# A hybrid decoder layer on one core: tile addresses, one wide value split, memory taken from two ends, and blocks staged through DRAM

## The chip, the core and the metric

The kernel runs on one core of one Trainium2 chip. The metric is the device time of one execution in microseconds (us). Three runs of the kernel before took 2890.93, 2891.61 and 2895.39 us; their median is 2891.61 us. The engines are PE (TensorE, with its weight loads shown as PEld), DVE (VectorE), ACT (ScalarE), POOL (GpSimd) and SP, which here only issues DMAs.

## The reference

One decoder layer on x of 2048 tokens by 1024, in float32:

```
u  = x * (1 + s1) + sh1                     # modulation vectors from c
qa, ka, va, qb, kb, vb, ga, gb = split(u @ w_in)
ya = banded attention, 8 heads, window 128, with sinks
yb = three dilated groups of 4 heads (dilation 1, 4, 16), mixed by their denominators
m  = (sigmoid(ga) * (ya @ w_a) + sigmoid(gb) * (yb @ w_b)) @ w_o
x1 = layer_norm(2**0.25 * x + g1 * m)
u2 = x1 * (1 + s2) + sh2
out = layer_norm(2**0.25 * x1 + g2 * ((silu(u2 @ w_gate) * (u2 @ w_up)) @ w_down))
```

w_gate and w_up are 1024 x 2816, w_down is 2816 x 1024.

## The kernel before, in words

Each float32 operand of a product is split into a high and a low part (`split`, L114: a copy on ScalarE, L115, then a subtraction on VectorE, L116), and each product is three matmuls (`PASS`, L141). PE works through five stages in one stream.

1. **The dilated groups** (L622 to L679). Four residue classes r, for each first the group of dilation 4 (g = 2), then that of 16. For g = 2 `project_v` (L553) makes the values of both groups at once, 4 PSUM banks of 512 columns (8 heads). `split_v` (L569) splits the first four heads of all four banks into three bfloat16 parts (`v_split`, L361: a ScalarE copy L364, then on VectorE L365, L366, L367); after that `send_v` (L578) splits the other four heads and stores them to DRAM, from where `fetch_v` loads them for the other group. The banks carry the name mm, of which there are four, and the next projection needs one.
2. **The near group and branch A** (L681 to L751), four chunks of 512 tokens.
3. **Merge, output projection, first layer norm** (L772 to L919), chunks in the order 3, 0, 1, 2. mT (pool mtp, L777) is the stationary operand of the output projection (L903). The rows x1 go to DRAM (x1_s).
4. **The first two products of the FFN** (L940 to L1130), in a Strassen form with seven products for each 2 x 2 block. Two passes p of 1024 tokens, in each eleven groups g of 256 columns, for each group one set of products with w_gate and one with w_up: 44 sets of 84 matmuls (L1014). `left(p, k)` (L956), for k = 0 to 3, loads four 512 x 128 blocks of x1, transposes them on PE (L967), modulates them on ScalarE (L968), forms four sums (`left_sums`, L928) and splits the seven blocks into comb tiles. `Right` (L976) loads 1 MB of weights (raw), forms four sums (`right_sums`, L934) and splits them into four units a to d, which replace the units of the set before as its products end. At the end of an up set `left_sums` runs on GpSimd over the four blocks of the gated result, and the seven blocks are stored to h_s (L1129, L1130). raw, sums, gated results and left blocks share one pool, g4, of six 1 MB tiles. The first and the last set of a pass (`set_by_block`, L1079) go block by block k, so that they can run while `left` makes the blocks.
5. **The product with w_down** (L1132 to L1268): seven products m in the order 1, 2, 6, 5, 3, 7, 4, eleven steps each; a step loads and splits one pair of factors (`factors`, L1147) and issues 24 matmuls (L1171) into eight banks. In the steps of m = 1 `right_of` (L1160) makes the sums of w_down and stores them to t_s. After m = 3 `first_half`, after m = 7 `second_half` (L1223, L1232) run one token block per step: the gate g2 on GpSimd (L1190), the residual (L1191), statistics and layer norm on VectorE. The last six factor pairs of m = 4 are held, and each block t is finished and stored on its own (L1265).

All DMAs are issued by SP, in order. The tile framework places each tile in its pool, the pools of a stage one after another from the low end of memory, makes an instruction that takes over a tile wait for the last user of the memory, and orders the work of each engine by its own estimate of when it is ready.

Of the kernel before, what the change touches and what calls it, by code (L numbers as in the profile page):

```python
# [23 lines left out]
KT = D // 128  # L24
# [28 lines left out]
def tile_pool(tc, name, bufs, stack):  # L53
    return stack.enter_context(tc.tile_pool(name=name, bufs=bufs, reuse_waits="tile"))
# [3 lines left out]
def trunk(ctx, tc, x, c, w_ada, b_ada, w_in, sinks, w_a, w_b, w_o, ln1_g, ln1_b,  # L58
# [17 lines left out]
    t_s = dram.tile([FT // 2, 4, 128, 512], F32, name="t_s")  # L76
# [15 lines left out]

    early = ctx.enter_context(ExitStack())
# [3 lines left out]
    ubp = early.enter_context(tc.tile_pool(name="ubp", bufs=UB))  # L97
    utp = early.enter_context(tc.tile_pool(name="utp", bufs=20))
    qp = early.enter_context(tc.tile_pool(name="qp", bufs=12))
# [261 lines left out]
    def v_split(pool, v, ps, nh, h0=0):  # L361
        pv = ps[:, h0 * 64:(h0 + nh) * 64].rearrange("p (h d) -> p h d", h=nh)
        r = pool.tile([128, 6, 64], F32, name="vr")[:, :nh]
# [37 lines left out]
    with ExitStack() as ph:  # L401
# [90 lines left out]
        vrp = pool("vrp", 1)  # L492
        att = pool("att", 3)
        at = Attention()
# [74 lines left out]
        def split_v(ps, nh):  # L569
            res = []  # L570
            for t in range(4):
                v = ring(vp, 8, [128, 6, 3, 64], BF16, "v")
# [5 lines left out]
        def send_v(ps, r):  # L578

            for t in range(4):  # L580
# [3 lines left out]
                nc.sync.dma_start(v_s[r, t * 128:(t + 1) * 128], v[:, :4].rearrange("p h a d -> p (h a d)"))  # L584

        def fetch_v(r):
            res = []
            for a in range(4):
                v = ring(vp, 8, [128, 6, 3, 64], BF16, "v")
# [32 lines left out]
        with ExitStack() as ph1:  # L622
            tab, osp, ada = pool("tab1", 1, ph1), pool("osp", 4, ph1), pool("ada", 1, ph1)
            vtp = pool("vtp", 2, ph1)
# [56 lines left out]
        with ExitStack() as ph2:  # L681
            tab, ogp, ytp = pool("tab2", 1, ph2), pool("ogp", 2, ph2), pool("ytp", 2, ph2)
            ptp = pool("pt2", PTB, ph2)
            at.phase = 1
            tA = bias_tables(tab, ubp, "tab", 127, [(h, 1) for h in range(8)])
# [85 lines left out]

    with ExitStack() as ph:  # L772
        ada = pool("ada3", 1, ph)
        tmp = pool("tmp3", 2, ph)
        ylp = pool("ylp", 4, ph)
        xrp = pool("xrp", 4, ph)
        mtp = pool("mtp", 16, ph)  # L777
        sgp = pool("sgp", 3, ph)
        later = ada_steps(ada, (S2, SH2, G2))
# [61 lines left out]

        yls, yT = [], []
        for _ in chain(y_rows(3, yls), y_T(yls, yT)):
            pass
        for ch, after in ((3, 0), (0, 1), (1, 2), (2, None)):
            mT, yls = [], []
            rows = y_rows(after, yls) if after is not None else iter(())
            for m in range(KT):
# [21 lines left out]
                if m >= 4:  # L870
# [10 lines left out]
            turn = [0, False]  # L881

            def bank():

                turn[0] += 1
                if turn[1]:
                    return psum.tile([128, 512], F32, name="mm")
                return psum.tile([128, 512], F32, name="so"[turn[0] % 2], bufs=2)

# [26 lines left out]
            for b in range(4):  # L916
                layer_norm(tmp, xr[b], sts[b], l1g, l1b)
                T = ch * 4 + b
                nc.sync.dma_start(x1_s[T * 128:(T + 1) * 128, :], xr[b])  # L919

    early.close()
    pool = partial(tile_pool, tc)
    A11, A12, A22, A_1, A_2, A_3, A_4 = range(7)
    G = FT // 2

    def left_sums(s, a11, a12, a21, a22, eng):  # L928
        eng.tensor_tensor(s[:, 0], a21, a22, op=OP.add)  # L929
        eng.tensor_tensor(s[:, 1], s[:, 0], a11, op=OP.subtract)  # L930
        eng.tensor_tensor(s[:, 2], a11, a21, op=OP.subtract)
# [362 lines left out]
```

## Time and profile before

| | |
|---|---|
| median of 3 runs | 2891.61 us |
| the profiled execution, time | 2895.43 us |
| its span, first to last instruction | 2893.4 us |
| granted TensorE clock, mean | 0.97 |
| PE busy | 2723.8 us |
| DVE busy | 1957.7 us |
| ACT busy | 1157.5 us |
| POOL busy | 254.9 us |
| HBM read, written | 325.94 MB, 94.97 MB |

The profile counts an engine as busy from the start of an instruction to its end; "idle before" is the engine's idle time just before an instruction and what released it. A granted clock of 1.00 is the full 2.4 GHz, one of 0.50 is 1.2 GHz; a stretch's number is its mean.

### The profile page before, as it was taken

The numbers are of one execution on the slowest core, as the hardware profiler recorded it, in microseconds if no ns is written. First come the engines' busy times: TensorE is split into PE (matmuls) and PEld (weight loads), VectorE is DVE, ScalarE is ACT, GpSimd is POOL, SyncE is SP. The second block draws the span as 40 slices with busy tenths as digits, with TensorE's granted clock in tenths as the row PEclk, the third lists the DMA queues.
The fourth block names the chain that finished last, engine by engine and source line by source line (L and its number), as shares of the span: only waits on it lengthen the run. The fifth ranks groups of instructions, "written<-read, shape, count | busy, mean of one in ns | idle before, by whom it ended". The sixth has DMA issues, their size and how long they took to land. (4 is left out here: it accounts for less than half of the span.)

```text
span 2893.4 us, 36361 instructions
## 1 busy us (share of the span) xinstructions
PE 2723.8 (94%) x13331; PEld 2232.6 (77%) x13331; DVE 1957.7 (68%) x3459; ACT 1157.5 (40%) x1918; POOL 254.9 (9%) x163
## 2 busy tenths in 40 slices
PE   7899999999999999999978999996999997999986
PEld 5677778888887888888856888885888886888875
DVE  7756677787769867655467666666666674543499
ACT  3544655666685343342224222233322222333220
POOL 0000000000000000000000111101111110000233
PEclk9999999999999999999989999997999998999998
DMA  9855857776788664734423233232332325974463
GB/s 282 227 154 143 212 143 165 153 171 146 167 223 269 212 182 129 229 120 153 126 80 97 97 109 104 93 117 86 109 107 97 110 95 218 325 266 150 136 221 125
DMA packets 570306, 459.23 MB, mean 159 GB/s; under 512 B 206152, under 2 KB 482704, under 8 KB 570128
## 3 DMA queue, kind: packets, MB, share of 16 engines
q1 hardware_dynamic: 570128, 456.92, 54.1%
q8 instruction: 104, 1.70, 0.2%
q14 instruction: 74, 0.61, 0.1%
HBM read 325.94 MB, written 94.97 MB: 145 GB/s over the span
## 5 line engine op out<-in xcount | busy, mean ns | idle before, releaser
L1014 PE MATMUL mm<-cb,w 128*128 128x512 f32 x3696 | 861.8, 395 | 31.4 <-ACT w L115 12.3
L1014 PEld LDWEIGHTS mm<-cb,w 128*128 128x128 f32 x3696 | 700.1, 190 | 184.5 <-ACT w L115 13.4
L148 PE MATMUL mm<-ut,whl 128*128 128x512 f32 x3072 | 736.2, 396 | 24.0 <-DVE vr L365 16.8
L148 PEld LDWEIGHTS mm<-ut,whl 128*128 128x128 f32 x3072 | 576.5, 190 | 156.0 <-issue 18.4
L1171 PE MATMUL acc<-hw 128*128 128x512 f32 x1848 | 427.2, 394 | 37.6 <-ACT hw L115 18.7
L1171 PEld LDWEIGHTS acc<-hw 128*128 128x128 f32 x1848 | 351.4, 191 | 113.4 <-ACT hw L115 29.5
L116 DVE TENSOR_TENSOR whl<-raw,whl 128x1024 fp32r<-128x1024 f32 (+1 forms) x228 | 265.5, 1165 | 164.6 <-ACT whl L115 162.9
L115 ACT ACTIVATE whl<-raw 128x1024 fp32r<-128x1024 f32 (+1 forms) x228 | 230.3, 1010 | 330.8 <-PE mm L148 78.4
L115 ACT ACTIVATE w<-g 128x1024 fp32r<-128x1024 f32 (+1 forms) x176 | 166.9, 951 | 367.6 <-PE mm L1014 329.3
L116 DVE TENSOR_TENSOR hw<-raw,hw 128x1536 fp32r<-128x1536 f32 x77 | 147.7, 1919 | 126.4 <-ACT hw L115 121.1
L115 ACT ACTIVATE hw<-raw 128x1536 fp32r<-128x1536 f32 x77 | 114.7, 1490 | 283.4 <-PE acc L1171 119.3
L116 DVE TENSOR_TENSOR w<-g,w 128x1024 fp32r<-128x1024 f32 (+1 forms) x176 | 194.4, 1107 | 37.9 <-ACT w L115 37.8
L1018 DVE TENSOR_TENSOR t<-mm,t 128x512 f32<-128x512 f32 x138 | 94.9, 688 | 134.3 <-PE mm L1014 134.3
L288 DVE TENSOR_TENSOR ehl<-te,ehl 128x512 f16<-128x512 f32 (+1 forms) x160 | 98.4, 615 | 111.9 <-ACT ehl L287 111.7
L561 PE MATMUL mm<-whl,ut 128*128 128x512 f32 (+1 forms) x768 | 160.2, 365 | 0.0
L561 PEld LDWEIGHTS mm<-whl,ut 128*128 128x128 f32 x768 | 137.4, 188 | 16.4
L148 PE MATMUL mm<-q,whl 128*128 128x512 f32 x576 | 137.8, 395 | 2.0 <-DVE q L116 1.3
L148 PEld LDWEIGHTS mm<-q,whl 128*128 128x128 f32 x576 | 109.8, 191 | 25.7 <-DVE q L116 1.5
L767 POOL TENSOR_TENSOR rs<-rs,mhalf 128x1 f32<-128x1 f32 x32 | 45.0, 1412 | 847.4 <-DVE rs L766 847.2
L929 POOL TENSOR_TENSOR g<-g 128x512 f32<-128x512 f32 x22 | 45.3, 2060 | 769.4 <-DVE g L1041 713.0
L277 DVE CUSTOM_DVE_ANT_0 te<-s,tab 128x256 f32<-128x256 f32 (+1 forms) x320 | 109.7, 383 | 1.0 <-PE s L265 0.7
L300 PE MATMUL o<-v,pt 128*128 128x192 bf16 x1096 | 91.5, 235 | 4.5 <-DMA pt<-ehl 4.4
(180 smaller groups left out, 2864.6 us busy)
## 6 DMA issues: line engine op xcount, KB each, us to landing
raw<-in_w_in_dram SPq DMA_DIRECT2D x132, 512.0 KB, 4.0
raw<-h_s SPq DMA_DIRECT2D x77, 512.0 KB, 3.8
g<-in_w_gate_dram SPq DMA_DIRECT2D x22, 1024.0 KB, 7.7
g<-in_w_up_dram SPq DMA_DIRECT2D x22, 1024.0 KB, 5.3
h_s<-g SPq DMA_DIRECT2D x22, 1024.0 KB, 5.1
h_s<-g SPq DMA_DIRECT2D x22, 768.0 KB, 3.5
raw<-in_w_ada_dram SPq DMA_DIRECT2D x32, 512.0 KB, 4.2
raw<-in_w_o_dram SPq DMA_DIRECT2D x32, 512.0 KB, 3.7
```

The source lines that it names most:

```text
L115: nc.scalar.activation(hi, src, AF.Copy)
L116: nc.vector.tensor_tensor(lo, src, hi.bitcast(F32), op=OP.subtract)
L148: nc.tensor.matmul(ps, lhs(k, a), rhs(k, b), start=i == 0, stop=i == n - 1)
L277: nc.vector.tensor_tensor_reduce(out=te[:, h, :nk], in0=ps[h], in1=tables[h][:, 256 - nk:], scale=1.0, scalar=-3e38, op0=OP.add, op1=OP.ma ...
L288: nc.vector.tensor_tensor(eh[:, 1], te[:, :, :nk], eh[:, 0], op=OP.subtract)
L300: nc.tensor.matmul(pv[:, h, a:], pt[:, (a * 2 + h) * nb + j], v[:, :3 - a], start=j == 0 and a == 0, stop=j == nb - 1 and a == 1)
L561: nc.tensor.matmul(ps[t][:, :n], lhs_of(us[k][a], t), whl[:, b, kk * n:(kk + 1) * n], start=k == 0 and i == 0, stop=k == KT - 1 and i == 2)
L767: nc.gpsimd.tensor_tensor(rs, rs, mhalf, op=OP.pow)
L929: eng.tensor_tensor(s[:, 0], a21, a22, op=OP.add)
L1014: nc.tensor.matmul(ps, r.of(m, k, a), us[k][b][:, LEFT[m]], start=first and k == 0 and i == 0, stop=last and k == 3 and i == 2, skip_group ...
L1018: nc.vector.tensor_tensor(out, ps, other, op=op)
L1171: nc.tensor.matmul(ps, hw[:, a, t * 128:(t + 1) * 128], hw[:, b, 1024:], start=first and i == 0, stop=last and i == 2, skip_group_check=True)
```

## The change

Six things change; the rest of the code stays.

- **Addresses.** Small pad tiles are added and pools reordered, so that the tiles that PE reads start at multiples of 128 bytes. In stage 3 mtp now stands ahead of the pool of small tiles (tmp3).
- **Values.** `split_v` splits all eight heads of a bank at once; `send_v` only stores.
- **Two ends.** The pools of the modulated x (ubp, utp), of q (qp) and, in stage 3, ada3 and ylp lie at the high end of memory. In the last chunk of stage 3 they are closed when the merge is done, and `open_right` loads, sums and splits the left blocks k = 0 and 1, loads k = 2 and the first weights and forms their sums, all ahead of the output projection. In the last set of stage 4 `open_down` does the same for the first factors of stage 5.
- **Transposed x1 through DRAM.** For chunks 3, 0 and 1 PE transposes x1 in stage 3, in the next chunk's loop (`turned`); for chunk 2 two calls of `turn` do it in stage 4. Left blocks are then loaded from xT_s.
- **Left blocks of pass two through DRAM.** In sets 11, 13, 15 and 17 the seven blocks of one k of pass two are made and stored to l_s (`left_ahead`); at the turn of the passes they are loaded and split. The first sets of a pass do products 1 to 7 over k = 0 and 1 first, then k = 2, then k = 3; the last sets do k = 0 and 1, then finish product by product.
- **Sums on VectorE, w_down ahead.** `left_sums` of the gated result moves from GpSimd to VectorE. w_down is multiplied by g2 and summed in stage 4 (`down_right`, sets 2, 6, ... 42), so stage 5 loads both factors ready and does not apply g2. In stage 5 the residual of the first half is split in two (`first_left` after m = 2, `first_right` after m = 3), and its statistics go to ScalarE.

g4 shrinks from six tiles to two; raw and the right sums get two tiles (g1) and the left blocks two (x1t).

```diff
-    vrp = pool("vrp", 1)
+    att.tile([128, 8], F32, name="pad", bufs=1)
...
-                v = vtp.tile([128, 6, 3, 64], BF16, name="vt")
-                with tc.high_priority(offset=EVICT):
-                    v_split(vrp, v, ps[t], 4, 4)
-                nc.sync.dma_start(v_s[r, t * 128:(t + 1) * 128], v[:, :4]...)
+            for t, v in enumerate(vs):
+                nc.sync.dma_start(v_s[r, t * 128:(t + 1) * 128], v[:, 4:]...)
...
-                        vv = split_v(ps, 4)
-                        send_v(ps, r)
+                        vv = split_v(ps, 8)
+                        send_v(vv, r)
...
+    def g1():
+        return gp.tile([128, 4, 512], F32, name="g1")
+    def x1t():
+        return gp.tile([128, 4, 512], F32, name="x1t")
+    def left_modulated(p, k):
+        e = x1t()
+        nc.sync.dma_start(e[:, 1:3], dr(xT_s, (k + 4) * 128 * S + p * 1024, ...))
+        for hf in range(2):
+            nc.sync.dma_start(e[:, 3 * hf], dr(xT_s, k * 128 * S + p * 1024 + hf * 512, ...))
+        for kk, i in ((k, slice(0, 1)), (k, slice(3, 4)), (k + 4, slice(1, 3))):
+            nc.scalar.activation(e[:, i], e[:, i], AF.Identity, scale=mod[:, S2, kk:kk + 1], ...)
+        return e
+    def left_load(p, k):
+        e, s = left_modulated(p, k), x1t()
+        left_sums(s, e[:, 0], e[:, 1], e[:, 3], e[:, 2], nc.vector)
+        return e, s
+    def left_again(k):
+        es = x1t(), x1t()
+        for i in range(2):
+            nc.sync.dma_start(es[i], dr(l_s, (k * 8 + i * 4) * 128 * 512, ...))
+        return es
+    def open_right():
+        gp = tile_pool(tc, "g1", 2, ctx, "right")
+        comb = tile_pool(tc, "comb1", 4, near, "right")
+        us01 = [left_split(left_load(0, k), comb) for k in range(2)]
+        raw0, t0 = load_right(w_gate, 0), g1()
+        gate_sums(t0, raw0)
+        es2 = left_load(0, 2)
+    def open_down():
+        rawp = tile_pool(tc, "raw5", 3, ctx, "right")
+        hwa = tile_pool(tc, "hwa", 3, ctx, "right")
+        ready = [factors(n) for n in range(AHEAD)]
...
+        def turned(ch, xr):
+            for k in range(KT):
+                ps = bank()
+                for b in range(4):
+                    nc.tensor.transpose(ps[:, b * 128:(b + 1) * 128], xr[b][:, k * 128:(k + 1) * 128], ident)
+                ub = ubp.tile([128, 512], F32, name="ub")
+                nc.scalar.activation(ub, ps, AF.Copy)
+                nc.sync.dma_start(xT_s[k, :, ch * 512:(ch + 1) * 512], ub)
+                yield
...
+            if after is None:
+                outer.close()
+                open_right()
...
+        def down_right(g):
+            b = x1t()
+            nc.sync.dma_start(v, dr(w_down, 2 * g * 128 * D, ...))
+            def scale():
+                for f in range(2):
+                    nc.vector.tensor_tensor(v[:, f], v[:, f], g2b, op=OP.mult)
+            def sums():
+                t = x1t()
+                right_sums(t[:, 0], ..., nc.vector)
+                for i, x in enumerate((t, b)):
+                    nc.sync.dma_start(dr(t_s, (g * 8 + i * 4) * 128 * 512, ...), x)
+        def left_ahead(k):
+            e = left_modulated(1, k)
+            def sums():
+                s = x1t()
+                left_sums(s, ..., nc.vector)
+                for i, x in enumerate((e, s)):
+                    nc.sync.dma_start(dr(l_s, (k * 8 + i * 4) * 128 * 512, ...), x)
...
+        def turnover(k):
+            nxt.append(left_split(es.pop(0), comb))
+            es.append(left_again(k + 1))
+        def second(k):
+            us.append(left_split(es.pop(0), comb2))
+            if k == 2:
+                es.append(left_again(3))
+        def leave(k):
+            if k == 1:
+                near.close()
+                open_down()
...
-                left_sums(s, h[:, C11], h[:, C12], h[:, C21], h[:, C22], nc.gpsimd)
+                left_sums(s, h[:, C11], h[:, C12], h[:, C21], h[:, C22], nc.vector)
...
-                w = xrp.tile([128, D], F32, name="xr")[:, :512]
-                nc.vector.tensor_tensor(w, ps, g2b[:, L], op=OP.mult)
-                nc.vector.tensor_tensor(x, x, w, op=OP.subtract)
+                nc.vector.tensor_tensor(x, x, ps, op=OP.subtract)
...
+        def first_right(t):
+            residual(y1[t], R, t, 0)
+            nc.scalar.activation(junk, y, AF.Copy, accum_out=mv[:, :1])
+            nc.scalar.activation(junk, y, AF.Square, bias=nm, accum_out=mv[:, 1:])
+            scale_add(y, mv, l2g, rs, l2b)
```

## Rows read from the trace of the kernel before

**Rows 1.** The page: busy time of the engines, and PE in 40 slices (tenths).

```profile
PE 2723.8 (94%) x13331; PEld 2232.6 (77%) x13331; DVE 1957.7 (68%) x3459; ACT 1157.5 (40%) x1918; POOL 254.9 (9%) x163
...
PE   7899999999999999999978999996999997999986
```

**Rows 2.** Stretches: length, busy PE, PEld, DVE, ACT, POOL; clock, DMA share, GB/s.

```profile
78.00:90.00 12.00, 2.39 (x7) 1.68 (x6) 10.69 (x22) 2.26 (x5) 0.00 (x0) 0.71 0.70 192
177.00:190.00 13.00, 9.04 (x35) 7.41 (x34) 7.98 (x20) 2.10 (x4) 0.00 (x0) 0.74 0.31 101
274.00:280.00 6.00, 2.39 (x8) 1.64 (x7) 5.48 (x14) 1.47 (x3) 0.00 (x0) 0.79 0.28 82
...
1480.00:1545.00 65.00, 38.03 (x152) 27.49 (x151) 48.72 (x59) 29.24 (x29) 5.42 (x4) 0.75 0.37 113
1545.00:1953.00 408.00, 407.58 (x1804) 335.42 (x1803) 275.90 (x323) 126.49 (x159) 71.67 (x40) 1.00 0.32 104
1953.00:2012.00 59.00, 36.38 (x125) 26.04 (x124) 43.61 (x47) 23.57 (x25) 7.28 (x4) 0.68 0.28 88
2410.00:2440.00 30.00, 11.28 (x39) 8.58 (x38) 15.94 (x18) 5.05 (x4) 5.41 (x4) 0.66 0.83 298
...
2790.00:2810.00 20.00, 10.07 (x34) 7.81 (x33) 18.77 (x22) 6.87 (x5) 3.49 (x3) 0.75 0.79 274
2835.00:2850.00 15.00, 6.07 (x19) 4.11 (x18) 15.00 (x12) 1.49 (x1) 4.71 (x4) 0.70 0.32 101
```

**Rows 3.** Timeline of stage 5, from 2785 us to the end.

```profile
2786.77 1.74 DVE L116 TENSOR_TENSOR hw<-raw,hw 128x1536 fp32r<-128x1536 f32 x1
...
2827.22 3.57 DVE L116 TENSOR_TENSOR hw<-raw,hw 128x1536 fp32r<-128x1536 f32 x1
...
2833.05 3.57 DVE L116 TENSOR_TENSOR hw<-raw,hw 128x1536 fp32r<-128x1536 f32 x1
...
2848.22 30.68 PE L1171 MATMUL acc<-hw 128*128 128x512 f32 x128 [4.12 <-DVE hw L116]
```

**Rows 4.** Timeline, 270 to 279 us: start, us, engine, line, operation, [idle before].

```profile
271.71 0.42 DVE L365 TENSOR_TENSOR vr<-mm,v 128x256 f32<-128x256 f32 x1
...
277.92 0.42 DVE L365 TENSOR_TENSOR vr<-mm,vt 128x256 f32<-128x256 f32 x1
...
278.48 0.77 PE L148 MATMUL mm<-ut,whl 128*128 128x512 f32 x1 [3.61 <-DVE vr L365]
```

**Rows 5.** Groups by form in the stretch 1545 to 1953 us: busy, mean ns.

```profile
L116 DVE TENSOR_TENSOR w<-g,w 128x1024 fp32r<-128x1024 f32 x63 | 76.9, 1221 | 19.0 <-ACT w L115 19.0
...
L1041 DVE TENSOR_TENSOR g<-t,g 128x512 f32<-128x512 f32 x31 | 32.3, 1042 | 0.7
...
L929 POOL TENSOR_TENSOR g<-g 128x512 f32<-128x512 f32 x10 | 21.5, 2152 | 349.2 <-DVE g L1041 349.2
...
L937 DVE TENSOR_TENSOR g<-g,g 128x512 f32<-128x512 f32 x20 | 13.6, 682 | 0.0
```

**Rows 6.** Timeline of PE: the output projection, and 46 us of stage 4.

```profile
1467.87 2.96 PE L903 MATMUL o<-whl,mT 128*128 128x512 f32 x12
1470.67 2.96 PE L903 MATMUL s<-whl,mT 128*128 128x512 f32 x12
...
1699.77 46.40 PE L1014 MATMUL mm<-cb,w 128*128 128x512 f32 x204
```

**Rows 7.** The page's DMA issues: count, KB each, median us from issue to landing.

```profile
g<-in_w_gate_dram SPq DMA_DIRECT2D x22, 1024.0 KB, 7.7
g<-in_w_up_dram SPq DMA_DIRECT2D x22, 1024.0 KB, 5.3
h_s<-g SPq DMA_DIRECT2D x22, 1024.0 KB, 5.1
```

**Rows 8.** Timeline of SP's queue in stage 4, around the start of a gate set.

```profile
1722.96 0.37 SPq L1129 DMA_DIRECT2D h_s<-g  x1
...
1726.27 0.46 SPq L981 DMA_DIRECT2D g<-in_w_gate_dram  x1
```

More of the change, by code (lines that the diff above doesn't have):

```diff
@@ new lines, in left_load, with left_split @@
+    def left_load(p, k):
[5 more added lines that the diff above has]
+        for i in range(2):
+            nc.sync.dma_start(es[i], dr(l_s, (k * 8 + i * 4) * 128 * 512, [[512, 128], [128 * 512, 4], [1, 512]]))
+        return es
+    def left_split(es, comb):
+        hi, lo = (comb.tile([128, 7, 512], F32R, name="cb") for _ in range(2))
+        split(hi[:, :3], lo[:, :3], es[0][:, :3])
+        split(hi[:, 3:], lo[:, 3:], es[1])
+        return hi, lo
@@ new lines, in open_right, with factors @@
+    def open_right():
+        nonlocal gp, comb, us01, es2, raw0, t0
+        gp = tile_pool(tc, "g1", 2, ctx, "right")
[4 more added lines that the diff above has]
+        es2 = left_load(0, 2)
+    gp = comb = us01 = es2 = raw0 = t0 = None
+    def factors(n):
+        m, g = steps[n]
+        raw = rawp.tile([128, 1536], F32, name="raw")
+        nc.sync.dma_start(raw[:, :1024], dr(h_s, (g * 7 + LEFT[m]) * 128 * 1024, [[1024, 128], [1, 1024]]))
+        nc.sync.dma_start(raw[:, 1024:], t_s[g, RIGHT[m]])
+        hw = (hwa if n % 7 < 3 else hwb).tile([128, 2, 1536], F32R, name="hw")
+        split(hw[:, 0], hw[:, 1], raw)
+        return hw
@@ L840, in y_T, with bank @@
                 yield
+        turn = [0, False]
+        def bank():
+            turn[0] += 1
+            if turn[1]:
+                return psum.tile([128, 512], F32, name="mm")
+            return psum.tile([128, 512], F32, name="so"[turn[0] % 2], bufs=2)
+        def turned(ch, xr):
[7 more added lines that the diff above has]
+                yield
+        behind = iter(())
         yls, yT = [], []
@@ L869, in trunk @@
                     next(later, None)
-                if m >= 4:
+                if m < 4:
+                    next(behind, None)
+                    next(behind, None)
+                else:
                     next(rows, None)
@@ new lines, in finish, with done, after @@
+        def finish(us, r, sink, then, ps, ks):
+            def done(m):
+                product(ps[m], m, us, r, ks, False, True)
+                return ps[m]
+            def after(m):
+                for f in then.get(m, ()):
+                    f()
+            m1, u2, u3 = small(), small(), small()
+            nc.scalar.activation(m1, done(1), AF.Copy)
+            after(1)
+            add(u2, done(6), m1)
+            after(6)
+            p = done(2)
+            sink.sum(C11, lambda t: add(t, p, m1))
+            after(2)
+            add(u3, done(7), u2)
+            after(7)
+            d = done(5)
+            sink.sum(C22, lambda t: add(t, d, u3))
+            v2 = small()
+            add(v2, d, u2)
+            after(5)
+            e = done(4)
+            sink.sum(C21, lambda t: add(t, u3, e, OP.subtract))
+            after(4)
+            c = done(3)
+            sink.sum(C12, lambda t: add(t, c, v2))
+            after(3)
@@ L1099, in trunk, with first @@
         sets = [(p, g, w) for p in range(2) for g in range(G) for w in (w_gate, w_up)]
-        rights = {n: Right(sets[n][2], sets[n][1]) for n in range(1)}
-        rights[0].sums()
+        rights = {0: Right(sets[0][2], sets[0][1], raw0)}
+        rights[0].sums(t0)
         for n in "abcd":
             rights[0].unit(n)
-        us = [left(0, k) for k in range(4)]
-        nxt = []
+        us = us01 + [left_split(es2, comb2)]
+        es3 = left_load(0, 3)
+        nxt, es = [], []
+        def first(k):
+            if k == 3:
+                us.append(left_split(es3, comb2))
```

318 lines of the change are left out of this document (164 added, 154 removed).

## The prediction

> **What bounds the kernel now.** I read the page first: PE is busy for 2723.8 of 2893.4 us and DVE for 68%, and PE's line of 40 slices is at 9 except at the start, near the middle, at slice 27, at slice 33 and at the end [rows 1]. PE is the bound, and since the change leaves PE the same matmuls, only time in which PE stands, or runs slowly, can be won. The stretches size that. In each I count as lost its length less PE's busy time at the granted clock: from 1480 to 1545 us (stage 3 to 4) 65.0 - 38.03 x 0.75 = 36.5 us; from 1953 to 2012 (pass one to two) 59.0 - 36.38 x 0.68 = 34.3; from 2410 to 2440 (stage 4 to 5) 30.0 - 11.28 x 0.66 = 22.6; after the value splits of stage 1 10.3, 6.3 and 4.1, and a fourth like the third, together 25 [rows 2]. At the end it is 12.4 at 2790, 10.8 at 2835 [rows 2] and 14.5 from the end of the last matmul (2848.22 + 30.68 = 2878.9) to the end of the span [rows 3], together 37.7. In sum 156 us. In between, from 1545 to 1953, PE is busy for 407.58 of 408 us at clock 1.00 [rows 2]: nothing can be won there, and whatever the change makes late there is a new loss.
>
> **The change, part by part.**
>
> *Values.* A bank of the next projection is released when all its heads have been read. In class 2 the first subtraction L365 starts at 271.71, the one that frees the first bank at 277.92, as fifth of eight splits, and PE waits 3.61 us for it [rows 4]. With one split of eight heads the first subtraction frees the bank. One of 512 columns takes 0.68 us by L937 [rows 5], so the bank is free at 272.4, before PE has finished at 278.48 - 3.61 = 274.9. The four waits should go; I leave 3 us of the 25 for the first class, where VectorE is late for another reason, and take 22 (15 to 25). Half as many splits, each wider, add nothing.
>
> *Addresses.* Twelve matmuls of the output projection are 1470.67 - 1467.87 = 2.80 us apart, 233 ns each; those of stage 4 take 46.40 / 204 = 227 ns [rows 6]. Both have 512 columns; what differs is that mT lies behind small tiles of 8 to 160 bytes. If the address is the reason, 768 matmuls x 6 ns = 5 us. I take 5 (0 to 8; other operands behind small tiles are the excess over 5). The Trainium skill speaks against it: its page "SBUF — State Buffer", section "Specifications (TRN2)", gives SBUF lines of 16 bytes and asks only for enough hits in each, which consecutive float32 give at any address; by it this term would be 0 and the sum 5 us later.
>
> *Stage 3 to 4.* Today all of `left` comes after the last layer norm. In the changed kernel the left blocks 0 and 1 and the first weights are ready before, during the 192 matmuls (45 us) of the last output projection. Not covered is k = 2, whose split takes memory from mT, and comes behind four layer norms on VectorE. A comb of 7 x 512 columns costs, at 1.74 us for 1536 [rows 3], 4.1 us. Layer norm by two passes of 1024 at about 1.2 us [rows 5] and small steps is some 2.9 us a block, 11.6 for four. PE has 42 x 0.227 = 9.5 us of products over k = 0 and 1 meanwhile: late by about 6. k = 3 can load only when the two x1t tiles are free: 5.1 us to land [rows 7], sums 4 x 0.68 [rows 5], split 4.1, against 21 x 0.227 = 4.8 us of products: late by about 8. I leave 14 of the 36.5 (2 to 20) and win 22.5.
>
> *Pass one to two.* 84 matmuls make a set of 19.05 us. The comb tiles of k = 0 are free 4.8 us into the last set; from there four blocks must be split until 19 + 9.5 + 4.8 = 33.3 us. A block costs the landing of a tile, 5.1 us [rows 7], and its half of the split, about 4 us with both engines, so 9; the first is loaded: 4.8 + 4 + 3 x 9 = 35.8, late by 2.5. VectorE's other work, 275.9 us in 21.4 sets, 12.9 a set [rows 2], takes part of that time; I leave 8 of the 34.3 (2 to 20) and win 26.3.
>
> *Stage 4 to 5.* Raw factors come into the memory of the first two comb tiles, free 4.8 to 9.5 us into the last set, and need a landing of about 5 us and a split of 1.74; 9.5 us of matmuls remain. I leave 3 of 22.6 (1 to 8) and win 19.6.
>
> *End.* From 2827.22 to 2833.05 a step of VectorE takes 5.83 us; the split in it takes 3.57 where it took 1.74 without GpSimd's gate beside it [rows 3]. Without the gate the step is about 4.1 us, below the 24 x 0.227 = 5.4 us of PE. In m = 7 the same holds: part of the residual is moved ahead and the statistics go to ScalarE. Of 12.4 + 10.8 I leave 4.5 (2 to 10). In the tail a multiplication less for each of eight blocks (0.68 [rows 5]) brings VectorE below PE's 18 x 0.227 = 4.1 us a block; the last block's norm and its store remain, I leave 8 of 14.5 (7 to 10). Won: 25.2.
>
> *What is added in stage 4.* VectorE gets 88 sums (0.68 each, 60 us) and, for eleven groups, two products of 1024 columns and four sums (about 5.1 us, 56 us). GpSimd no longer disturbs it: L1041 takes 1042 ns instead of about 0.68 with GpSimd's 2152 ns sums beside it [rows 5]. In the stretch 1545 to 1953 that is 275.9 + 10.7 x 2.7 + 5.4 x 5.1 - 31 x 0.36, about 320 of 408 us: no bound. `turned` and `turn` replace PE's 128 transposes one for one; 32 ScalarE copies and some 40 DMAs are hidden by engines with room (ScalarE 126 of 408 [rows 2]); I take 3 us for waits they add (0 to 6). The 24 residual loads instead of 16 and the four x1 stores through GpSimd's queue lie beside PE work and cost nothing unless SP stands.
>
> *The queue.* This is the real cost. With six tiles, raw weights for a set were issued at 1726.27 [rows 8], more than 30 us ahead of their products. With two, the load of a set waits for the last unit split of the set before, some 2.4 us into a set; SP takes it after the stores before it. An ordinary load lands 5.3 to 7.7 us later [rows 7]; sums and the first unit (4 x 0.68 + 2 x 1.22 [rows 5]) make 15 of 19.05: 4 us to spare. In eleven sets 2 MB of stores to t_s, in four sets 2 MB to l_s and the stores of h_s are ahead of it; at 5.1 us for 1 MB the load then lands at 17 to 19 us, and its first unit is 3 to 5 us late: 11 x 3 + 4 x 5 = 53 us if SP keeps the order, 0 if the loads go first, which the framework can choose. I take 15 (0 to 53), nearer to the lower end, because SP's order in the rows follows readiness closely.
>
> **Sum.** 22 + 5 + 22.5 + 26.3 + 19.6 + 25.2 = 120.6 won, 3 + 15 = 18 lost: 102.6 us less than the profiled execution's 2895.4, 2792.8. That execution is 3.8 us above the median of three, 2891.6; taken in the middle of both the forecast is 2790.
>
> **Rivals.**
>
> *The loads are late in the fifteen sets.* All 53 us are paid: 2895.4 - 120.6 + 56 = 2831. For it: SP stood before L1129 and took L981 right behind it [rows 8]. Against: ready loads can be put first.
>
> *The turns close only half.* Of the 93.4 us of the three turns 47 remain instead of 25: 2815. For it: each block makes a way to DRAM and back, with 5 us of landing, where two tiles serve.
>
> *The early work is not early.* The memory at the high end may not be free in time, or VectorE and ScalarE may get the work late in their order, and the change does not do what it says at the turns: only 22 + 5 + 25.2 - 18 remain, 2861. Against: the last user of that memory is the last gate of the merge, 45 us before the turn.
>
> *All turns close and no load is late.* Then only the tail and some 4 us remain: 2750.
>
> *Slower: two raw tiles starve every set.* One mechanism, in the steady stretch: the load of each of 42 sets begins only when the set before has given up its tile, and its landing stands in the path. The 4 us to spare are used up if it lands 11 to 12 us after its issue instead of 7.7; with x us late in each set the loss is 42x, and it decides from 117.6 / 42 = 2.8 us. With 5 us late everywhere it would be 2988. For it: nothing else is as tight; eight banks bridge only some three products. Against: the weights of a gate set landed in 7.7 us behind 1.75 MB of stores already [rows 7, 8].
>
> **How the numbers follow.** Forecast (2770 to 2812) 0.53; late loads in fifteen sets 0.15; half-closed turns 0.10; all closed 0.08; early work not early 0.06; slower 0.06; no change, by losses that happen to meet the gains, 0.02. The range 2750 to 2845 takes in the first four; outside are the last three and the far ends of the others, about 0.2. Faster by over 0.2% (about what a measurement of this kernel can tell from no change, 6 us): 0.53 + 0.15 + 0.10 + 0.08 + 0.06 = 0.92. Same 0.02, slower 0.06.
>
> **What would show it.** In the profile after: no wait of PE on L365 in stage 1; 227 ns between matmuls of the output projection; PE's slices at 9 where the three turns are, with k = 3 as the last wait in each; POOL nearly idle from stage 4 on; VectorE's factor split at 1.74 throughout stage 5; the last matmul about 8 us before the end. Gaps of 3 to 5 us at the start of the sets after 2, 6, 10, ... would show the late loads. The prediction is wrong if gaps stand in every set, or if the turns still have 20 us each.

## The result, and the profile after

The changed kernel takes 2793.64 us, median of 4 runs (2789.55 to 2796.16), against 2891.27 (2889.24 to 2895.39): a ratio of 0.9659, 95% interval 0.9642 to 0.9676. The forecast was 2790. The profiled execution took 2794.94 us, 100.5 less than the profiled one of before.

The page of the kernel after (busy time of the engines, and PE in 40 slices), against [rows 1]:

```profile
PE 2695.8 (97%) x13331; PEld 2217.4 (79%) x13331; DVE 1925.6 (69%) x3513; ACT 1183.5 (42%) x1956; POOL 56.6 (2%) x63
...
PE   7999999999998999999998999998999999999998
```

PE is busy for 28 us less with the same 13331 instructions. 4.6 us of it are the output projection (189.2 us in PE's groups by form before, 184.6 after); the rest fits fewer matmuls at the lower clock, as the turns below are at 0.89 to 0.91 where [rows 2] had 0.66 to 0.75. The slices below 9 that are left, counted from 1 (the prediction counts from 0), are the start, the end of stage 2 (slice 13), stage 3 to 4 (22), pass one to two (28) and the end.

The stretches after, in the columns of [rows 2] (the first value split, stage 3 to 4, the steady stretch, pass one to two, stage 4 to 5):

```profile
78.00:90.00 12.00, 10.02 (x51) 8.02 (x52) 11.42 (x17) 6.29 (x8) 0.00 (x0) 0.92 0.84 239
...
1465.00:1525.00 60.00, 46.66 (x172) 35.57 (x171) 50.01 (x65) 20.96 (x22) 7.81 (x8) 0.89 0.36 123
1525.00:1925.00 400.00, 397.15 (x1761) 327.09 (x1760) 292.45 (x396) 134.60 (x168) 0.00 (x0) 1.00 0.55 190
1925.00:1985.00 60.00, 48.94 (x188) 36.83 (x187) 47.53 (x61) 17.76 (x20) 0.00 (x0) 0.89 0.63 217
...
2350.00:2370.00 20.00, 16.15 (x65) 12.88 (x63) 19.21 (x21) 8.71 (x6) 0.00 (x0) 0.91 0.84 281
```

By the measure of the prediction (length less busy PE times clock) the turns lose 60 - 46.66 x 0.89 = 18.5, 60 - 48.94 x 0.89 = 16.4 and 20 - 16.15 x 0.91 = 5.3 us. They lost 36.5, 34.3 and 22.6 before. The first value split still loses 12 - 10.02 x 0.92 = 2.8 us; at the other three PE is busy without a gap at clock 1.00.

Where PE stands in the first two turns, in the timelines of PE, VectorE, ScalarE and SP of the kernel after:

```profile
1471.24 2.53 ACT L120 ACTIVATE w<-g 128x1024 fp32r<-128x1024 f32 x3 [14.38 <-PE o L1028]
...
1479.72 1.17 DVE L121 TENSOR_TENSOR w<-g,w 128x1024 fp32r<-128x1024 f32 x1
...
1480.95 3.58 PE L1144 MATMUL mm<-cb,w 128*128 128x512 f32 x8 [5.18 <-DVE rs L770]
...
1485.72 2.96 DVE L121 TENSOR_TENSOR w<-g,w 128x1024 fp32r<-128x1024 f32 x3
...
1486.99 11.21 PE L1144 MATMUL mm<-cb,w 128*128 128x512 f32 x41 [2.46 <-DVE w L121]
...
1489.54 3.96 DVE L121 TENSOR_TENSOR cb<-x1t,cb 128x1536 fp32r<-128x1536 f32 x2 [0.87 <-DMA x_s<-xr]
...
1932.11 0.37 SPq L1071 DMA_DIRECT2D x1t<-in_w_down_dram  x1
...
1934.91 0.36 SPq L838 DMA_DIRECT2D x1t<-l_s  x1
...
1943.52 1.48 ACT L120 ACTIVATE cb<-x1t 128x1536 fp32r<-128x1536 f32 x1 [14.67 <-DMA x1t<-l_s]
...
1945.05 4.72 PE L1144 MATMUL mm<-cb,w 128*128 128x512 f32 x9 [8.01 <-ACT cb L120]
...
1946.82 0.36 SPq L838 DMA_DIRECT2D x1t<-l_s  x1
```

In the first turn the data k = 0 and 1 are there, but the weight units are not: ScalarE's copies for them wait 14.38 us for the output projection (o, L1028), and VectorE makes the first low part at 1479.72 and the other three at 1485.72, between the layer norms. (The wait of 5.18 us is put down to L770, a small step of a layer norm that ends at the same time as the first low part.) In the second, a w_down pair takes one of the two x1t tiles at 1932.11, and the two halves of k = 3 are loaded through the other, 12 us apart.

The end, in the timeline of PE, the factor splits of VectorE in the groups by form, and two blocks of the tail in VectorE's timeline:

```profile
2684.84 96.27 PE L1338 MATMUL acc<-hw 128*128 128x512 f32 x424
...
L121 DVE TENSOR_TENSOR hw<-raw,hw 128x1536 fp32r<-128x1536 f32 x77 | 135.2, 1757 | 176.5 <-ACT hw L120 172.6 <-DMA raw<-t_s 3.7
...
2774.78 1.28 DVE L764 SCALAR_TENSOR_TENSOR y<-y,rs,x1t 128x1024 f32<-128x1024 f32 x1 [0.44 <-POOL rs L771]
...
2779.45 1.28 DVE L764 SCALAR_TENSOR_TENSOR y<-y,rs,x1t 128x1024 f32<-128x1024 f32 x1 [0.44 <-POOL rs L771]
```

424 matmuls stand in one group that ends at 2781.1, so PE has no gap there, where [rows 3] had waits. The span goes on for 12.1 us after it. In this tail one block takes VectorE 4.67 us (from one row of L764 to the next), of which 0.44 us is a wait for a small step on GpSimd.

The loads of raw weights in the page's DMA issues, against [rows 7]:

```profile
g<-in_w_gate_dram SPq DMA_DIRECT2D x22, 1024.0 KB, 6.4
g<-in_w_up_dram SPq DMA_DIRECT2D x22, 1024.0 KB, 5.4
```

From issue to landing they take about as long as before, with two tiles instead of six.

### The profile page after: what moved, and what is told of

The parts are those of the page before. It is cut to its first block, busy times and chain, and to the rows that moved or that the text cites. A ratio compares the mean times of both kernels' runs of the same rounds, so it can differ in the third digit from the quotient of the medians.

```text
span 2793.2 us, 36324 instructions
## 1 busy us (share of the span) xinstructions
PE 2695.8 (97%) x13331; PEld 2217.4 (79%) x13331; DVE 1925.6 (69%) x3513; ACT 1183.5 (42%) x1956; POOL 56.6 (2%) x63
## 4 chain that ended last, share of the span: by engine, by line
PE 64%; DVE 5%; DMA 4%; issue 1%; ACT 1%; POOL 0%; SPq 0%; DVEq 0%; ACTq 0%; POOLq 0%
PE mm L1144 25%; PE mm L153 16%; PE acc L1338 14%; PE mm L1028 3%; PE s L1028 1%; PE o L1028 1%; PE o L305 1%; DMA x1t<-xT_s 1%; PE s L270 1%; PE mm L566 1%; DMA sg<-s_s 1%; DMA x1t<-l_s 1%; DVE cb L121 1%; POOL rs L771 0%; DMA sty<-st_s 0%
## 5 line engine op out<-in xcount | busy, mean ns | idle before, releaser
L1144 PE MATMUL mm<-cb,w 128*128 128x512 f32 x3696 | 855.0, 393 | 27.2 <-ACT cb L120 10.2
L1338 PE MATMUL acc<-hw 128*128 128x512 f32 x1848 | 420.8, 390 | 3.9 <-DVE t L1148 3.9
L121 DVE TENSOR_TENSOR hw<-raw,hw 128x1536 fp32r<-128x1536 f32 x77 | 135.2, 1757 | 176.5 <-ACT hw L120 172.6
L566 PEld LDWEIGHTS mm<-whl,ut 128*128 128x128 f32 x768 | 137.4, 188 | 16.4
L292 ACT ACTIVATE ehl<-te 128x512 f16<-128x512 f32 (+1 forms) x160 | 89.8, 561 | 12.7 <-DMA pt<-ehl 10.5
L305 PEld LDWEIGHTS <-pt 128*128 128x128 f16 x1096 | 75.1, 99 | 25.2 <-issue 18.8
```

The source lines that it names most:

```text
L121: nc.vector.tensor_tensor(lo, src, hi.bitcast(F32), op=OP.subtract)
L292: nc.scalar.activation(eh[:, 0], te[:, :, :nk], AF.Copy)
L305: nc.tensor.matmul(pv[:, h, a:], pt[:, (a * 2 + h) * nb + j], v[:, :3 - a], start=j == 0 and a == 0, stop=j == nb - 1 and a == 1)
L566: nc.tensor.matmul(ps[t][:, :n], lhs_of(us[k][a], t), whl[:, b, kk * n:(kk + 1) * n], start=k == 0 and i == 0, stop=k == KT - 1 and i == 2)
L1144: nc.tensor.matmul(ps, r.of(m, k, a), us[k][b][:, LEFT[m]], start=first and k == 0 and i == 0, stop=last and k == 3 and i == 2, skip_group ...
L1338: nc.tensor.matmul(ps, hw[:, a, t * 128:(t + 1) * 128], hw[:, b, 1024:], start=first and i == 0, stop=last and i == 2, skip_group_check=True)
```

## The experiments

Totals hide a stretch here: in twelve profiles of these kernels the last matmuls of stage 3 start between 1462.0 and 1477.5 us (leaving out the first experiment, which changes stage 1), although these kernels differ little up to there. So stage 4 and 5 are compared by marks, read off the timelines of PE: A, the start of the last matmul of the output projection; B, the first transposition of `turn` in set 4; C, the first matmul of stage 5; D, the end of the last one; E, the end of the span.

```
run                     A       A-B      B-C     C-D     D-E
after                 1470.8   116.8    772.7   420.8   12.1
e2_addr32             1473.4   117.4    771.5   420.7   12.1
e8_after_again        1470.1   115.9    772.4   420.7   12.1
e3_late_left          1472.3   116.2    771.8   421.7   12.6
e4_late_down          1470.4   116.2    768.3   419.7   12.1
e5_wd24               1466.6   116.1    765.4   420.8   12.1
e6_place              1477.5   111.4    772.3   422.0   12.2
e7_best               1468.5   111.9    760.7   419.7   12.1
e9_order              1476.9   111.2    760.7   419.7   12.3
e10_mirror            1473.5   139.5    772.8   420.8   12.6
e11_gate5             1462.0   116.3    770.7   428.6   15.0
e12_queue             1474.3   116.8    769.7   420.8   11.7
```

In the kernels whose edit does not touch it, A to B lies between 115.9 and 117.4 us, B to C between 771.5 and 772.8, C to D between 420.7 and 422.0. Where no count is given, an experiment is a single run; the eight runs of the changed kernel lie between 2789.55 and 2799.33 us.

**The value splits undone.**

```diff
-                    v_split(vrp, v, ps[t], nh)
+                    v_split(vrp, v, ps[t], min(nh, 6) if nh < 8 else 4)
...
             for t, v in enumerate(vs):
+                with tc.high_priority(offset=EVICT):
+                    v_split(vrp, v[:, 4:], ps[t], 4, 4)
```

> The changed kernel with the value splits of class 2 undone: each 512-wide bank is read in two parts of four heads again, the four first parts of all banks ahead of the four second parts. Theory (a bank is free only when its last head has been read): PE waits for the subtraction of v_split again in each of the four classes, the first stage ends 20 to 22 us later, and the execution takes 2794.9 + 21 = 2816 us (2810 to 2820). Rival (stage 1 gained by the memory moved, the split width is hidden): the time stays within 4 us of 2794.9 and no wait on v_split appears.

Measured: 2817.69 us, 22.8 more than 2794.94. PE's waits by group, 60 to 460 us, of this run:

```profile
L153 PE MATMUL mm<-ut,whl 128*128 128x512 f32 x768 | 195.6, 411 | 19.7 <-DVE vr L370 17.0 <-DVE ut L121 2.2 <-DVE mod L207 0.4
L205 PE MATMUL mm<-ones,adacc 128*128 128x1 f32 x16 | 3.5, 351 | 3.6 <-DVE vr L370 3.6
```

The subtraction holds PE for 17.0 + 3.6 us again; in the kernel after it was 0.3, in the kernel before 16.8 + 3.6 (L365, in PE's waits). So the width of the split is the gain, and the memory moved has no visible part in this wait.

**The operand 32 bytes off.**

```diff
+        pool("mpad", 1, ph).tile([128, 8], F32, name="mpad")
         mtp = pool("mtp", 16, ph)
```

> The changed kernel with the stationary operand of the output projection (mT) moved up by 32 bytes, off the multiples of 128; the moving operand (the weights) stays where it was. Theory of the prediction (an address off 128 bytes costs 6 ns a matmul of 512 columns): 12 matmuls of the output projection start 2.80 us apart again instead of 2.72, 768 of them cost 5 us, 2800 us in all. Rival (lines of 16 bytes, as the Trainium skill has them on its page SBUF — State Buffer, in Specifications (TRN2)): 32 bytes change nothing, the spacing stays 2.72 us and the time within 2 us.

Measured: 2796.76 us. The output projection in PE's timeline and groups by form, first of the kernel after, then of this run:

```profile
1465.60 2.88 PE L1028 MATMUL s<-whl,mT 128*128 128x512 f32 x12
1468.32 2.88 PE L1028 MATMUL o<-whl,mT 128*128 128x512 f32 x12
...
L1028 PE MATMUL mm<-whl,mT 128*128 128x512 f32 x384 | 92.4, 394 | 2.0 <-DVE sg L990 2.0
L1028 PE MATMUL s<-whl,mT 128*128 128x512 f32 x192 | 46.1, 389 | 0.0
L1028 PE MATMUL o<-whl,mT 128*128 128x512 f32 x192 | 46.1, 389 | 0.0
```

```profile
1467.99 2.96 PE L1029 MATMUL s<-whl,mT 128*128 128x512 f32 x12
1470.79 2.96 PE L1029 MATMUL o<-whl,mT 128*128 128x512 f32 x12
...
L1029 PE MATMUL mm<-whl,mT 128*128 128x512 f32 x384 | 94.2, 399 | 0.8 <-DVE sg L991 0.8
L1029 PE MATMUL o<-whl,mT 128*128 128x512 f32 x192 | 47.4, 396 | 0.0
L1029 PE MATMUL s<-whl,mT 128*128 128x512 f32 x192 | 47.4, 396 | 0.0
```

The 768 matmuls are busy for 189.0 us against 184.6: 4.4 us, by the address alone; groups of twelve start 2.80 us apart, as in [rows 6], instead of 2.72. The total moved by 1.8 us, which single runs can't resolve.

**The left blocks late, in the text.**

```diff
-            if after is None:
-                outer.close()
-                open_right()
...
     early.close()
+    outer.close()
+    open_right()
```

> The changed kernel with the left blocks 0 to 2 and the first weights of stage 4 prepared after the last layer norm instead of before the last output projection; nothing else is moved. Theory (the early work is what the third turn of memory bought): the stretch between stage 3 and 4 loses 30 to 38 us again instead of 18.5, the time is 2794.9 + 16 = 2811 us (2806 to 2816). Rival (the wait for layer norms and k = 3 hides it): within 4 us of 2794.9.

Measured: 2796.34 us, A to B 116.2. The number that the rival gave came, but not for its reason: the edit did not do what it says. ScalarE still splits a left block 27 us before A, in this run's timeline:

```profile
1445.38 1.47 ACT L120 ACTIVATE cb<-x1t 128x1536 fp32r<-128x1536 f32 x1
```

Here the work went where its memory and data allow it, not where the text has it. The exchange of the two ends of the memory, below, takes the memory itself away.

**The factors of stage 5 late, in the text.**

```diff
-            if k == 1:
-                near.close()
-                open_down()
+            pass
...
+    near.close()
+    open_down()
     with ExitStack() as ph:
         y1p = pool("y1p", 8, ph)
```

> The changed kernel with the first factors of stage 5 loaded and split after the last set instead of inside it. Theory (they lie beside the last half set's products): the stretch between stage 4 and 5 loses about 22 us instead of 5.3, the time is 2794.9 + 16 = 2811 us (2804 to 2816). Rival (the tiles of the last residual products hide it, or the gain came from the sums on w_down ahead): within 4 us of 2794.9.

Measured: 2788.45 us, faster by 6.5; both expectations fell. PE's first group of stage 5 in the kernel after, and then in this run, from the timelines:

```profile
2360.34 11.86 PE L1338 MATMUL acc<-hw 128*128 128x512 f32 x44 [3.85 <-DVE t L1148]
```

```profile
2354.89 5.85 PE L1338 MATMUL acc<-hw 128*128 128x512 f32 x25
```

The wait of 3.85 us for an eviction (`t`) is gone. The loads still lie beside the last half set (SP issues the first at 2345.33). What the text changed is their rank: VectorE had three splits of 1.75 us among the last evictions, which free the banks of stage 5 (at 2353.06, 2355.57 and 2357.84), and now has one (at 2351.61). B to C is shorter by 4.4 us, C to D by 1.1.

**One w_down pair moved out of the turn.**

```diff
-            if n % 4 == 2:
-                scale, sums = down_right(n // 4)
+            if n % 4 == 2 and n != 22 or n == 24:
+                scale, sums = down_right(5 if n == 24 else n // 4)
```

> The changed kernel with one load moved: the sixth pair of w_down tiles is taken in set 24, behind the turn between the passes, instead of in set 22, in the middle of it. Theory (in set 22 it holds one of the two x1t tiles until its sums are done, so that the two halves of k = 3 go through the other tile one after the other): the gap of 8.4 us in the last set of pass one before k = 3 goes to 1 us or less, the stretch between the passes loses 8 to 10 us less than 16.4, and the execution takes 2786 us (2784 to 2789). Rival (the landing of l_s or the width of the split sets that wait): the gap stays over 6 us and the time within 2 us of 2794.

**The memory of k = 2, and the order of VectorE, between stage 3 and 4.**

```diff
-        tmp = pool("tmp4", 5, ph)
-        comb2 = pool("comb2", 4, ph)
+        comb2 = pool("comb2", 2, ph)
+        comb3 = pool("comb3", 2, ph)
+        tmp = pool("tmp4", 5, ph)
...
+        with tc.high_priority(offset=60):
             for n in "abcd":
                 rights[0].unit(n)
             us = us01 + [left_split(es2, comb2)]
```

> The changed kernel with the stage between 3 and 4 mended in two ways: the split block k = 2 gets memory of its own that lies under mT instead of under the four x1 rows (two pools of two tiles instead of one of four), and the four weight units and the split of k = 2 are put ahead of the last layer norms in VectorE's order. Theory (VectorE's order and that memory are what the stretch still loses): the gaps of 5.6 and 2.9 us go to under 2, the four small ones before k = 3 remain in part; the stretch loses 8 to 11 us instead of 18.5 and the execution takes 2786 us (2783 to 2789). Rival (k = 3's loads through the two x1t tiles set the end of the stretch whatever comes before): the sum of the gaps stays over 14 us, 2792 to 2795.

**The three together, and the base again.**

> All three together: the w_down load moved behind the turn, the memory and order between stage 3 and 4 as in the run before, and the factors of stage 5 called for after the last set (which by the run with that alone changed the order of the evictions, not the place of the loads: 2788.5). Theory (the three stretches are far apart and add up): 8.5 + 8 + 6.5 us less than 2794.9, 2772 us (2768 to 2778). Rival (what one stretch gains the next gives back): 2782 or more.

> The changed kernel once more, as the base of the three runs before it: 2793 us (2789 to 2797) by both theories; a difference from this value over 4 us would mean that the chip, not the edits, makes the differences.

Measured, all four on one chip, 4 runs each: the pair moved 2791.63 us (ratio to the kernel before 0.9633, 0.9604 to 0.9663), the order 2795.37 (0.9646, 0.9626 to 0.9666), the three together 2778.64 (0.9587, 0.9566 to 0.9609), the changed kernel again 2795.5 (0.9651, 0.9627 to 0.9675). Only the three together stand clear of the base; the first two miss their forecast of 2786, and the three come just outside theirs (2768 to 2778). The marks are finer. The pair moved takes 7.0 us off B to C (772.4 to 765.4); PE's wait before k = 3 is shorter, but not under 1:

```profile
1934.85 0.96 PE L1144 MATMUL mm<-cb,w 128*128 128x512 f32 x3 [2.91 <-ACT cb L120]
```

So the tile was most of that gap; the rest, the landing of the halves and their splits by the expectation's rival, was not tried apart. The order and the memory together take 4.5 to 5.4 us off A to B, about half of what was expected. The waits of 5.18 and 2.46 us are gone, and one takes their place, before k = 3:

```profile
1480.11 14.81 PE L1145 MATMUL mm<-cb,w 128*128 128x512 f32 x64 [0.34 <-DVE w L121]
1506.80 3.78 PE L1145 MATMUL mm<-cb,w 128*128 128x512 f32 x8 [11.88 <-DVE cb L121]
```

The three add up: B to C falls by 11.7, A to B by 4.0, C to D by 1.0 against the base again.

**k = 3 ahead of the layer norms too.** The run before, with `left_split(left_load(0, 3), comb3)` in the same block, and memory for it that no x1 row touches:

```diff
-        w8 = pool("w8", 4, ph)
+        w8 = pool("w8", 3, ph)
...
+        w8d = pool("w8d", 1, ph)
...
             us = us01 + [left_split(es2, comb2)]
-        es3 = left_load(0, 3)
+            us.append(left_split(left_load(0, 3), comb3))
```

> The version of the three mends once more, with the split of k = 3 put ahead of the layer norms as well and with no tile of k = 2 and k = 3 under the x1 rows (the fourth weight unit, which needs half a tile, gets a place of its own). Theory (what was left in the stretch, a gap of 12.3 us before k = 3, is VectorE going through four layer norms between its loads and its split: from 1477.6 to 1492.5 in that run): the gap goes to about 4 us (loads there at 1480.1, ScalarE 2.7, sums 2.6, low split 4.0, so 1489.5 against 1485.5), the time falls by 8 against the run of the three mends, ratio to the kernel before 0.956. Rival (the way of k = 3 through the two x1t tiles takes that long by itself): the gap stays over 10 us, ratio 0.959.

Measured: 2775.18 us, median of 5, ratio 0.9581 (0.9568 to 0.9594): the fastest version here, but not apart from the run of the three mends. A to B is 111.2 against 111.9. PE's timeline shows why:

```profile
1495.51 0.98 PE L1147 MATMUL mm<-cb,w 128*128 128x512 f32 x3 [1.73 <-DVE rs L770]
1498.97 6.29 PE L1147 MATMUL mm<-cb,w 128*128 128x512 f32 x14 [2.48 <-DVE cb L121]
...
1509.42 2.93 PE L1147 MATMUL mm<-cb,w 128*128 128x512 f32 x6 [3.02 <-DVE w L121]
```

The one wait of 11.9 us before k = 3 is two of 1.7 and 2.5, so the layer norms and the memory under their rows, changed together here, were its cause. But of these 7.7 us A to B keeps 0.7, and the 8 us expected of the total did not come: the weights of the next set are now behind the layer norms (3.02 us in the last row), and the rest went into small waits after it that were not followed. In the 40 us after A, the stretches of the run of three mends and of this run:

```profile
1468.70:1508.70 40.00, 26.66 (x105) 21.14 (x105) 37.68 (x47) 18.88 (x19) 6.68 (x8) 0.83 0.36 131
```

```profile
1477.00:1517.00 40.00, 31.30 (x109) 23.96 (x108) 38.00 (x49) 18.43 (x19) 10.24 (x8) 0.83 0.51 171
```

VectorE is busy for 37.68 and 38.00 of 40 us. By this reading it bounds the turn now, and its order only chooses who waits; no run with less work on VectorE was made.

**The two ends of the memory exchanged.**

```diff
-        gp = tile_pool(tc, "g1", 2, ctx, "right")
-        comb = tile_pool(tc, "comb1", 4, near, "right")
+        gp = tile_pool(tc, "g1", 2, ctx)
+        comb = tile_pool(tc, "comb1", 4, near)
...
-        pool = partial(tile_pool, tc)
+        pool = partial(tile_pool, tc, side="right")
         w8 = pool("w8", 4, ph)
```

> The changed kernel with the two ends of the memory exchanged in stage 4: the left blocks and x1t lie at the low end, where the weights and mT of the last output projection are in use until its last matmul, and the weight units lie at the high end, which is free 45 us earlier. No operation is added or left out. Theory (not the place in the program but the memory decides when the left blocks can be made: moving the text alone cost 1.4 us): the stretch between stage 3 and 4 loses 30 to 40 us instead of 18.5, 2806 to 2816 us. Rival (the layer norms and the second half of the blocks set the end anyway): within 4 us of 2794.9.

Measured: 2820.76 us, above the theory's range; A to B is 139.5, 22.7 more than after. The first weights wait too, since their raw tiles also lie at the low end, so the 22.7 us belong to both. PE's timeline of the turn:

```profile
1481.63 0.80 PE L1143 MATMUL mm<-cb,w 128*128 128x512 f32 x1 [7.73 <-ACT cb L120]
1495.04 5.33 PE L1143 MATMUL mm<-cb,w 128*128 128x512 f32 x13 [12.61 <-DVE cb L121]
```

The text is that of the late left blocks; only the ends differ, and 23 us with them. The memory at the high end is what makes the left blocks and the first weights early.

**The gate g2 back in stage 5.**

```diff
-                    nc.vector.tensor_tensor(v[:, f], v[:, f], g2b, op=OP.mult)
...
+            nc.gpsimd.tensor_tensor(y[:, hs], y[:, hs], g2b[:, hs], op=OP.mult)
             nc.vector.scalar_tensor_tensor(y[:, hs], xr, ALPHA, y[:, hs], op0=OP.mult, op1=OP.add)
...
+                nc.vector.tensor_tensor(ps, ps, g2b[:, L], op=OP.mult)
                 nc.vector.tensor_tensor(x, x, ps, op=OP.subtract)
```

> The changed kernel with the gate g2 put back where it was: multiplied in stage 5, on GpSimd for the residuals and on VectorE for the last product, and not on w_down. Theory (GpSimd's product beside VectorE makes the split of the factors slow and the multiplication lengthens the tail): 48 splits take over 3 us again, PE loses 8 to 20 us at the end of m = 3 and m = 7, the tail is 13 to 15 us instead of 12.1: 2806 to 2818 us. Rival (the residuals moved ahead and the statistics on ScalarE made the room, the gate itself is hidden): within 4 us of 2794.9, tail aside.

Measured: 2794.33 us in all, as the rival has it, but this execution reached A 8.8 us earlier. By the marks stage 5 takes 7.8 us more up to the last matmul and 2.9 more behind it: 10.7. PE's timeline, and VectorE and GpSimd beside each other at the wait, in this run:

```profile
2741.56 2.34 POOL L1358 TENSOR_TENSOR y<-y,g2b 128x1024 f32<-128x1024 f32 x1 [3.43 <-DVE y L1415]
...
2742.01 3.50 DVE L121 TENSOR_TENSOR hw<-raw,hw 128x1536 fp32r<-128x1536 f32 x1
...
2745.57 32.01 PE L1337 MATMUL acc<-hw 128*128 128x512 f32 x128 [4.79 <-DVE hw L121]
```

The split takes 3.50 us where GpSimd's product runs beside it. So do five more of the 77, at 3.57 or 3.58; two take 2.8, and the median is 1757 ns. The expectation had 48 such splits; the kernel before has seven, all at 3.5 to 3.6. The Trainium skill has this rule, on its page "GPSIMD Engine Reference", section "1. Specifications": GpSimd shares its SBUF interfaces with VectorE, whose instructions with two SBUF inputs contend; the row agrees. The wait returns beside the second half's residuals only, as in [rows 3]. Before, PE also waited 9.9 us for the evictions at the end of m = 7, where VectorE was behind with the first half:

```profile
2804.62 33.01 PE L1171 MATMUL acc<-hw 128*128 128x512 f32 x133 [9.93 <-DVE y L1211]
```

This wait stays away without the gate's move, so other parts of the change won it: the residual moved ahead and the statistics on ScalarE lie there, and which of them it was, was not tried apart.

**The stores to t_s doubled.**

```diff
-                    nc.sync.dma_start(dr(t_s, (g * 8 + i * 4) * 128 * 512, [[512, 128], [128 * 512, 4], [1, 512]]), x)
+                    for d in (t_s, t_two):
+                        nc.sync.dma_start(dr(d, (g * 8 + i * 4) * 128 * 512, [[512, 128], [128 * 512, 4], [1, 512]]), x)
```

> The changed kernel with the stores to t_s made twice, the second time to a DRAM array that nothing reads: 4 MB instead of 2 MB in each of eleven sets, 8.8 us more of transfers by the 4.4 us that 1 MB takes. Theory (SP takes the loads of the next set ahead of these stores, so nothing waits for them but the x1t tiles): the steady stretch stays at 397 of 400 us, the time within 3 us of 2794.9; only in the turn between the passes, where a w_down pair holds an x1t tile, some 2 us more. Rival (the prediction's term: the stores stand in the way of the weights, late by 3 to 5 us in these sets): 11 x 4 to 9 us, 2840 us or more.

Measured: 2795.05 us, 0.1 more than after. The steady stretch of this run:

```profile
1525.00:1925.00 400.00, 399.04 (x1776) 330.05 (x1775) 295.29 (x400) 134.37 (x169) 0.00 (x0) 1.00 0.63 217
```

2 MB more in each of eleven sets cost nothing. (The expectation's 4.4 us for 1 MB is no median: such a store to t_s lands 4.9 us after its issue by the page of the kernel after.) SP's queue in the kernel after shows the order behind it: the load of the next set goes ahead, h_s follows at the start of a set, t_s in its middle:

```profile
1568.62 0.37 SPq L810 DMA_DIRECT2D g<-in_w_up_dram  x1
1571.02 0.37 SPq L1325 DMA_DIRECT2D h_s<-g  x1
...
1587.43 0.37 SPq L810 DMA_DIRECT2D g<-in_w_gate_dram  x1
...
1598.79 5.22 SPq L1081 DMA_DIRECT2D t_s<-x1t  x2
```

## Why the prediction was right, and where not

The sum was 102.6 us of gain and the profiled executions differ by 100.5. Most terms hold, but the total owes its closeness to luck: two pairs of misses cancel, the turns against the queue, and two parts of the end against each other.

*Values* (22 predicted). Undone they cost 22.8 by single runs, with 20.6 of it in PE's wait on the subtraction. Right, and for the reason given; the 3 us left for the first class are 2.8.

*Addresses* (5). 4.4 us on the 768 matmuls. The size and the place of the cause are as predicted. By the Trainium skill's rule ("SBUF — State Buffer", "Specifications (TRN2)": lines of 16 bytes) it would have been 0; 32 bytes are two such lines, and the spacing changed, so the measurement decides.

*Stage 3 to 4* (14 left, 18.5 measured). The step that failed is "the left blocks 0 and 1 and the first weights are ready before". The blocks were, and the exchange of the ends shows why. Of the weights only the raw tiles and sums were; their splits need memory that the last output projection holds, and VectorE's place among the layer norms, 5.18 + 2.46 us of PE's wait. I had counted only k = 2 and k = 3 as late. A second cause is in the row at 1489.54: the low parts of k = 2 waited for the store of x1 rows, so their tile lay under these rows, which I had not looked up.

*Pass one to two* (8 left, 16.4 measured). The step by which a block costs "the landing of a tile" and "its half of the split" took two x1t tiles for granted. A w_down pair held one of them in that very set. I had counted its sums as load on VectorE, not its tile; 7 us go with it.

*Stage 4 to 5* (3 left, 5.3 measured). The factors were in time, as worked out; the early splits themselves delayed the evictions that free the banks.

*End* (12.5 left, 12.1 measured). The sum is right by luck. The waits before the tail were to leave 4.5 us and leave none. The tail was to be 8 us (7 to 10) and is 12.1: the step that failed is that a multiplication less "brings VectorE below PE's 18 x 0.227 = 4.1 us a block". A block takes VectorE 4.67 us, so it falls behind by 0.6 us with each. And the reason for the waits is half right: by the run with the gate put back the gate is worth 10.7 of the 25.6 won. I had both reasons in the text and gave them no shares.

*The queue* (15 lost). Nothing: SP takes the loads first, the lower end of my range, which I had named and not taken. The turns lose 18.5 + 16.4 + 5.3 = 40.2 instead of 25, the queue 0 instead of 15; that is why the sum is so close. Of the rivals the half-closed turns came nearest (40.2 of their 47 us); starved loads did not, with PE busy for 397.15 us of 400 and no wait for a weight load among its gaps from 1525 to 1900 us.

The terms as measured, 22.8 + 4.4 + 18.0 + 17.9 + 17.3 + 25.6 = 106.0, are 5.5 above the difference of the executions. The marks tell where it lies. The last matmuls of the output projection before, and the first transpositions of `turn` after, in PE's timelines:

```profile
1479.07 2.96 PE L903 MATMUL o<-whl,mT 128*128 128x512 f32 x12
```

```profile
1587.61 1.91 PE L1104 MATMUL mm<-ident,x1t 128*128 128x128 f32 x16
```

A comes at 1481.6 before and at 1470.8 after, 10.8 us earlier, though values and addresses, both ahead of A, are worth 27.2. Some 11 of the 16.4 us between are the 96 transpositions that `turned` moves ahead of A (an estimate, from sixteen in 1.91 us); they are won again behind it. The other 5 us are lost ahead of A, where the profiles of nearly equal kernels lie 15 us apart; their cause stays open. Of the signs named, two did not come: slices at 9 at the first two turns, and a last matmul 8 us before the end.

## What to carry to other kernels

Work that lies ahead of a turn is early only if its memory is, so read what held each byte before; where a schedule follows readiness, moving the lines of a program may move nothing. A tile pool shared by two purposes is a queue: list every holder of its tiles through the critical stretch. And where several causes could return one wait, give each its share before the change, or the total will be right by chance.

## What was not expected of the hardware

Kernels with nearly the same instructions reach the end of stage 3 anywhere between 1462.0 and 1477.5 us. The granted clock from 60 to 880 us is 0.99 in the earliest and 0.98 in the latest of these profiles, with PE busy 792.57 and 791.87 us; 0.01 of 820 us is some 8 of the 15, an estimate from two rounded figures. What makes the clock differ was not tried. And 32 bytes in the address of the stationary fp32r operand are enough to cost 6 ns on 227 in each matmul of the output projection; no other offset was tried.
